# A decoder layer on one core: x split while it loads, products scaled by token after PSUM, paced loads, and the mixer's last sums kept in PSUM

## The chip, the core and the metric

One core of one Trainium2 chip runs the whole layer in one launch. TensorE (PE) multiplies, with results in PSUM; VectorE (DVE), ScalarE (ACT) and GpSimd (POOL) work beside it; transfers are issued from SyncE's queue (SP) and from POOL's. Each engine takes its own instructions in the order that the program fixed, and waits at an instruction until what it needs is there. The metric is the device time of one execution in microseconds (us), as the median of several runs.

## The reference, cut

256 tokens of width 2048, all weights float32:

```
a = rms_norm(x, g_mix_pre);  proj = a @ w_in          # 2048 -> 3*1024 + 2*1024
q, k, v: 8 heads of 128, causal attention over one block of 256, ALiBi bias
conv: val * sigmoid(gate) -> depthwise conv(31) -> LayerNorm -> silu    # 1024 channels
mixed = concat(attn, conv) @ w_out
h = x + rms_norm(mixed, g_mix_post)
f = square(relu(rms_norm(h, g_ffn_pre) @ w_ff1)) @ w_ff2               # 2048 -> 8192 -> 2048
out = h + rms_norm(f, g_ffn_post)
```

## The kernel before, in words

**Products.** All weights stream through SBUF once, in chunks of 128 x 1024 words (`load_raw`, 512 KB, four buffers `raw`). `load_w` splits a chunk into a high part `whi` (ACT, line 123) and the rest `wlo` (DVE or POOL, line 125: `low_engines` says whose turn it is), seven buffers each; activations are split in the same way, and a product is three passes, high by high, low by high and high by low. `group_cols` makes 256 columns with the weights stationary, in four chunks (lines 190 and 197); `group_rows` makes 512 columns with the tokens stationary (lines 133, 136, 137). Each group has one of two accumulators in PSUM (`acc`, tile `mm`); a third use waits until the first was read out. Smaller PSUM tiles come from four banks `aux`.

**The clock of the program.** `tick` is called after each chunk. `later(n, ...)` puts work n ticks ahead; between, each tick takes some "fillers" (`rate`), which are the 240 taps of the depthwise convolution on DVE (line 410). A scheduler then fixes the order on each engine.

**Stages.** (1) x comes in transposed, in nine pieces (`x_piece`), each with the weights of the first two column groups (gate and value of the first conv channels). These two groups multiply the unsplit `xg` = x times gain by unsplit float32 weights (`mm_words`, line 216), and so does the third group (`group_words`). Meanwhile POOL sums the squares of x. (2) `x_columns` makes the two token factors r_x, `token_rows` turns them into a row `Rx` over all tokens, and `split_x` scales xg by Rx and splits it into `xa`, of which the other groups live. (3) Five more conv groups, then twice (q, k, q, k, v) with `scores`, `weights_t`, `values` some ticks later (`ppt`: transposes of the attention weights `sc`), with the taps under it all. At the end LayerNorm and silu (`ln_1`, `ln_2`). (4) The output projection: three groups of 512 columns over the attention half of `ma`, then three over the conv half, whose sums stay in `part` (SBUF), multiplied by the gain on POOL. (5) The fourth column group, with all of the first 128 tokens (t = 0) ahead of the second 128 (t = 1): `mix_scale` makes the factor of the norm and adds each of four column blocks to `xs` (`hidden`, line 601), and `hidden_t` transposes these (`pt`, line 609) and splits them into `ha`. The transposes stand between the matmuls of the six chunks that were held back for t = 1 (`TURN_FIRST`). (6) `first_cols` starts the feed-forward with t = 0 alone for six chunks (`TURN_SECOND` places the transposes of t = 1 there), then comes the rest: four quarters of w_ff1 and w_ff2.

POOL also issues three kinds of transfer: `gains` (4 x 256 KB), all of x as `xs` (2 MB) and `gbc_ffn` (1 MB).

Of the kernel before, what the change touches and what calls it, by code (L numbers as in the profile page):

```python
# [38 lines left out]
def tile_hybrid_layer(  # L39
# [73 lines left out]

    def load_w(nk, width):
# [104 lines left out]
    def group_words(a):  # L219
        ps = acc()  # L220
        for c in range(KD // 4):
            mm_words(ps, a, 4 * c, 4, c == 0, c == KD // 4 - 1)
            tick()
        return ps[:, :, :S]

# [93 lines left out]

# [5 lines left out]
    def x_piece(k0, nk):  # L325
        at, to = KD + k0 * S if k0 else 0, KD + (k0 + nk) * S
        tc.keep_in_program_order(nc.sync.dma_start(xraw[:, at:to], xt[:, at:to]))
        v = xraw[:, to - nk * S:to].rearrange("p (k s) -> p k s", k=nk)
        for j in range(nk):
            nc.vector.tensor_scalar_mul(xg[:, k0 + j, :], v[:, j, :], xraw[:, k0 + j:k0 + j + 1])  # L330
# [19 lines left out]
    def x_columns():  # L350
        p = aux("pss")
# [89 lines left out]
    later(1, split_x)  # L441
# [17 lines left out]
    def head_cols(ps, scale, tag):  # L459
        return merged(ph1, ps, ph1.tile([P, 2, S], F32, tag=tag, name=tag), scale)  # L460

    def scores(pair, qT, kT, pT):
# [19 lines left out]
        later(3, weights_t, sc, pT)  # L482
# [36 lines left out]
    def ln_2():  # L519
# [15 lines left out]
        with tc.issue_after(last.ins):
            nc.scalar.activation(warm, eps4, AF.Sqrt)
        for b in range(4):
            split(ma, GC + 2 * b, 2, ysq[:, 2 * b:2 * b + 2, :])
# [9 lines left out]
    for half in range(2):  # L548
        pTs = []
        for b in range(2):  # L550
            qT = head_cols(group_cols(xa), HD ** -0.5, "qT")
            kT = head_cols(group_cols(xa), 1.0, "kT")
# [5 lines left out]
        nc.scalar.activation(v, ps, AF.Copy)  # L558
# [6 lines left out]
    for n in range(4):  # L565
        nc.gpsimd.dma_start(gains[n], g_mix_post[:, n * G:(n + 1) * G].to_broadcast([P, G]))
# [19 lines left out]
    part.append(mg)  # L586
# [73 lines left out]
    def first_done(ps):  # L660
# [4 lines left out]
        nc.gpsimd.dma_start(gbc_ffn, g_ffn_post.to_broadcast([P, D]))  # L665
# [69 lines left out]
RATE = (2, 5, 4)  # L735
GATE_AT = 5
# [4 lines left out]
TURN_SECOND = ((), (), (), (0,), (1,), (2, 3))  # L741
# [79 lines left out]
```

## Time and profile before

| | |
|---|---|
| median of 3 runs | 1067.19 us (1066.45 to 1068.17) |
| the profiled execution | 1066.0 us |
| its span, first to last instruction | 1064.2 us |
| PE busy / DVE / ACT / POOL | 1048.5 / 662.4 / 500.9 / 227.6 us |
| granted TensorE clock over the span | 0.998 |
| read from HBM | 199.39 MB, 189 GB/s over the span |

The span and some 2 us around it make the profiled execution's time. A busy PE is a PE with a matmul under way, by ends that are modelled; what it waited for stands in the view of waits.

### The profile page before, as it was taken

To read this page: it belongs to the slowest core of one execution; us is meant where nothing else is said; L and a number is where in the kernel's file an instruction comes from. 1 tells how busy PE (TensorE), PEld (TensorE's weight loads), DVE (VectorE), ACT (ScalarE), POOL (GpSimd) and SP (SyncE) were. 2 spreads that over 40 slices of the span, in tenths; PEclk is the share of its full clock that TensorE was granted. 3 is DMA by queue.
4 is the path that set the end of the run, shared out by engine and by line. 5 is a ranking of instruction groups with operands and counts; after the bars stand their busy time and mean duration, and the time that the engine had idled before them with its cause. 6 is when DMAs were issued, how large, how long until landed. Compare 5 with 4: busy or idle time off the path is not lost.

```text
span 1064.2 us, 14143 instructions
## 1 busy us (share of the span) xinstructions
PE 1048.5 (99%) x5424; PEld 896.1 (84%) x5424; DVE 662.4 (62%) x855; ACT 500.9 (47%) x646; POOL 227.6 (21%) x148
## 2 busy tenths in 40 slices
PE   9999999999999999999999999999999999999996
PEld 8888888888787988888888888888888888888886
DVE  4579999866465776644466654556665546656554
ACT  0465455468455754444445443344443334444450
POOL 6699755300025310000001100000010000100111
PEclk9999999999999999999999999999999999999999
DMA  7667645554764565655566655656656555566642
GB/s 226 219 216 234 219 146 191 185 173 140 285 195 137 199 214 196 195 190 190 193 194 184 194 187 194 196 184 195 194 181 196 197 192 186 190 190 194 189 149 79
DMA packets 58403, 202.41 MB, mean 190 GB/s; under 512 B 6496, under 2 KB 8416, under 8 KB 57952
## 3 DMA queue, kind: packets, MB, share of 16 engines
q1 hardware_dynamic: 57600, 197.32, 57.4%
q0 software_dynamic: 736, 4.19, 1.1%
q8 instruction: 42, 0.69, 0.2%
q14 instruction: 25, 0.20, 0.0%
HBM read 199.39 MB, written 2.10 MB: 189 GB/s over the span
## 4 chain that ended last, share of the span: by engine, by line
PE 85%; DVE 6%; POOL 3%; ACT 3%; DMA 2%; issue 2%; DVEq 0%; ACTq 0%; POOLq 0%
PE mm L190 25%; PE mm L133 14%; PE mm L137 14%; PE mm L136 14%; PE mm L197 13%; PE mm L216 3%; POOL wlo L125 3%; DVE yp L410 3%; DMA raw<-in_weights_dram 2%; DVE wlo L125 1%; DVE xs L601 1%; ACT whi L123 1%; PE half L137 0%; PE half L136 0%; PE half L133 0%
## 5 line engine op out<-in xcount | busy, mean ns | idle before, releaser
L125 DVE TENSOR_TENSOR wlo<-raw,whi 128x1024 fp32r<-128x1024 f32 x299 | 382.4, 1280 | 288.3 <-ACT whi L123 287.9
L123 ACT ACTIVATE whi<-raw 128x1024 fp32r<-128x1024 f32 x356 | 376.0, 1058 | 383.6 <-PE mm L137 216.6
L190 PE MATMUL mm<-ha,whi 128*128 128x512 f32 (+1 forms) x1072 | 317.8, 385 | 0.0
L197 PEld LDWEIGHTS mm<-ha,wlo 128*128 128x128 f32 x1024 | 186.4, 188 | 40.4
L197 PE MATMUL mm<-ha,wlo 128*128 128x256 f32 x1024 | 197.1, 279 | 0.0
L136 PE MATMUL mm<-wlo,ua 128*128 128x512 f32 x496 | 193.0, 389 | 0.0
L133 PE MATMUL mm<-whi,ua 128*128 128x512 f32 x496 | 193.0, 389 | 0.0
L137 PE MATMUL mm<-whi,ua 128*128 128x512 f32 x496 | 193.0, 389 | 0.0
L190 PEld LDWEIGHTS mm<-ha,whi 128*128 128x128 f32 x1072 | 164.3, 189 | 2.9 <-DVE mg L596 0.2
L650 POOL TENSOR_TENSOR rl<-rl 128x512 f32<-128x512 f32 x32 | 39.4, 1231 | 570.6 <-ACT ua L649 570.6
L125 POOL TENSOR_TENSOR wlo<-raw,whi 128x1024 fp32r<-128x1024 f32 x57 | 139.2, 2462 | 50.3 <-ACT whi L123 44.7
L190 PE MATMUL mm<-xa,whi 128*128 128x512 f32 x416 | 129.9, 397 | 0.0
L410 DVE SCALAR_TENSOR_TENSOR yp<-yx,cols,yp 128x256 f32<-128x256 f32 x240 | 105.8, 483 | 6.2 <-ACT yp L406 3.0
L137 PEld LDWEIGHTS mm<-whi,ua 128*128 128x128 f32 x496 | 93.1, 188 | 19.4
L136 PEld LDWEIGHTS mm<-wlo,ua 128*128 128x128 f32 x496 | 93.1, 188 | 19.3
L133 PEld LDWEIGHTS mm<-whi,ua 128*128 128x128 f32 x496 | 93.1, 188 | 19.2
L197 PEld LDWEIGHTS mm<-xa,wlo 128*128 128x128 f32 x416 | 76.2, 188 | 17.0
L197 PE MATMUL mm<-xa,wlo 128*128 128x256 f32 x416 | 80.2, 279 | 0.0
L190 PEld LDWEIGHTS mm<-xa,whi 128*128 128x128 f32 x416 | 64.8, 189 | 1.2
L254 ACT ACTIVATE tb<-mm 128x512 f32<-128x512 f32 x45 | 26.8, 596 | 72.4 <-PE mm L190 72.4
L133 PE MATMUL mm<-whi,ma 128*128 128x512 f32 x128 | 50.2, 394 | 2.3 <-ACT part L573 2.3
L257 DVE SCALAR_TENSOR_TENSOR z<-mm,tb 128x512 f32<-128x512 f32 x37 | 25.6, 691 | 39.6 <-ACT tb L254 39.6
(168 smaller groups left out, 793.1 us busy)
## 6 DMA issues: line engine op xcount, KB each, us to landing
raw<-in_weights_dram SPq DMA_DIRECT2D x360, 512.0 KB, 4.1
raw<-in_weights_dram SPq DMA_DIRECT2D x14, 256.0 KB, 3.3
xs<-in_x_dram POOLq DMA_DIRECT2D x1, 2048.0 KB, 9.7
xraw<-in_xt_dram SPq DMA_DIRECT2D x7, 256.0 KB, 3.9
gains<-in_g_mix_post_dram POOLq DMA_DIRECT2D x4, 256.0 KB, 5.0
gbc_ffn<-in_g_ffn_post_dram POOLq DMA_DIRECT2D x1, 1024.0 KB, 4.9
out_dram<-fp SPq DMA_DIRECT2D x8, 128.0 KB, 2.0
out_dram<-fp SPq DMA_DIRECT2D x4, 256.0 KB, 2.3
```

The lines of the kernel that those rows point to most:

```text
L123: nc.scalar.activation(hi[:, :n], raw, AF.Copy)
L125: low_engines[0][chunks[0] % len(low_engines[0])].tensor_sub(lo[:, :n], raw, hi[:, :n].bitcast(F32))
L133: m = nc.tensor.matmul(ps, h, wh[:, j, :], start=first and j == 0, stop=False)
L136: nc.tensor.matmul(ps, h, wl[:, j, :], start=False, stop=False)
L137: nc.tensor.matmul(ps, l, wh[:, j, :], start=False, stop=last and j == nk - 1)
L190: m = nc.tensor.matmul(o[:, :, tok], wh[:, j, b * P:(b + 1) * P], a[:, ak + j, :, tok], start=st, stop=en)
L197: nc.tensor.matmul(ps[:, b, :S], wl[:, j, b * P:(b + 1) * P], a[:, ak + j, 0, :], start=False, stop=False)
L216: nc.tensor.matmul(ps[:, b, :S], w[:, j, b * P:(b + 1) * P], a[:, ak + j, :], start=first and j == 0, stop=last and j == nk - 1)
L254: nc.scalar.activation(tb, ps[:, :, S:], AF.Copy, scale=scale)
L257: nc.vector.scalar_tensor_tensor(z, ps[:, :, :S], scale, tb, op0=ALU.mult, op1=ALU.add)
L410: nc.vector.scalar_tensor_tensor(yp[0][:, b, :], hpad[:, g + b, k:k + S], tap_col(g + b, k), yp[0][:, b, :], op0=ALU.mult, op1=ALU.add)
L650: nc.gpsimd.tensor_mul(t, t, t)
```

## The change

**x.** Each piece is now split as it comes in, into the high and low part of x times gain, without the token factor (`high` on ACT, `low` on DVE; xg itself moves to ACT from the third block on). `split_x` is gone. Since the token factor is the same for all rows of a product's column, every product of xa is multiplied by Rx after it left PSUM: `scaled` merges the two halves of a group into a PSUM tile `zt` and `by_token` multiplies this by Rx into SBUF. The v groups, which have tokens on partitions, take r_x as ACT's scale. The two `z` copies of the first groups go to `zt` tiles too.

**Third group.** `group_words` is gone; the gate of the second pair of conv blocks goes through `group_cols` like the others, on split weights.

**Loads.** `gains`, `xs` and `gbc_ffn` are issued on SP's queue among the weights, in pieces of 256 KB, one every few ticks.

**Mixer.** `part` of t = 0 is copied to three PSUM banks (`pc0`), from which `hidden` reads; the last block is multiplied by its gain in place in PSUM, and `hidden` reads it there, for both halves of the tokens.

**Order.** The LayerNorm's last step and silu come in two halves, a tick apart (`swish`); `weights_t` comes after 4 ticks instead of 3; filler rates 5 and 4 become 4.7 and 3.7; POOL takes 4 low parts of 5 instead of 3 of 4 in the attention stage; the transposes of t = 1 stand a chunk later.

```diff
+    def by_token(zt, tag="z", bufs=3):
+        z = ph1.tile([P, 2, S], F32, tag=tag, name=tag, bufs=bufs)
+        nc.vector.tensor_mul(z, zt, over(Rx, 2))
+        return z
+    def scaled(ps, scale=1.0, **kw):
+        return by_token(merged(ph1, ps, aux("zt").rearrange("p (b s) -> p b s", b=2), scale), **kw)
...
         for j in range(nk):
-            nc.vector.tensor_scalar_mul(xg[:, k0 + j, :], v[:, j, :], xraw[:, k0 + j:k0 + j + 1])
+            if k0 < 2:
+                nc.vector.tensor_scalar_mul(xg[:, k0 + j, :], v[:, j, :], gains[j])
+            else:
+                nc.scalar.activation(xg[:, k0 + j, :], v[:, j, :], AF.Copy, scale=gains[j])
+        for j in range(nk):
+            high(xa, k0 + j, v[:, j, :], gains[j], slice(0, S))
+        for j in range(nk):
+            low(xa, k0 + j, v[:, j, :], gains[j], slice(0, S))
...
-    def split_x():
-        R = token_rows(r_x, Rx)
-        for k in range(0, KD, 2):
-            xn = aux("xn").rearrange("p (k s) -> p k s", k=2)
-            nc.vector.tensor_mul(xn, xg[:, k:k + 2, :], over(R, 2))
-            split(xa, k, 2, xn)
...
-    ps = group_words(xg)
-    z = ph1.tile([P, 2, S], F32, tag="z", name="z", bufs=3)
-    nc.vector.tensor_mul(z, ps, over(Rx, 2))
-    low_engines[0], rate[0] = (nc.gpsimd,), RATE[1]
+    rate[0] = RATE[1]
     for i in range(1, 4):
-        sig = gate_out(z if i == 1 else merged(ph1, group_cols(xa)), 2 * i)
-        value_out(merged(ph1, group_cols(xa)), 2 * i, sig)
-    low_engines[0], rate[0] = (nc.vector, nc.gpsimd, nc.gpsimd, nc.gpsimd), RATE[2]
+        zg = scaled(group_cols(xa))
+        low_engines[0] = (nc.gpsimd,)
+        sig = gate_out(zg, 2 * i)
+        value_out(scaled(group_cols(xa)), 2 * i, sig)
+    low_engines[0], rate[0] = (nc.vector,) + 4 * (nc.gpsimd,), RATE[2]
...
-        nc.gpsimd.dma_start(gains[n], g_mix_post[:, n * G:(n + 1) * G].to_broadcast([P, G]))
+        later(2 * n + 10, load, gains[n], g_mix_post[:, n * G:(n + 1) * G].to_broadcast([P, G]))
...
-    nc.gpsimd.dma_start(xs, x2.rearrange("(t p) d -> p t d", p=P))
+    for n in range(8):
+        t, cs = n // 4, slice(n % 4 * G, (n % 4 + 1) * G)
+        later(n + 6, load, xs[:, t, cs], x2[t * P:(t + 1) * P, cs])
...
+        first_half.append(aux("pc0"))
+        nc.scalar.activation(first_half[c], pc[:, 0, :], AF.Copy)
...
         for c in range(3):
-            hidden(t, r, c)
-        tc.keep_in_program_order(nc.vector.tensor_mul(mg[:, t, :], ps, gains[3]))
-        hidden(t, r, 3)
+            hidden(t, r, c, part[c][:, t, :] if t else first_half[c])
+        tc.keep_in_program_order(nc.vector.tensor_mul(ps, ps, gains[3]))
+        hidden(t, r, 3, ps)
...
-RATE = (2, 5, 4)
-GATE_AT = 5
+RATE = (2, 4.7, 3.7)
+GATE_AT = 3
-TURN_SECOND = ((), (), (), (0,), (1,), (2, 3))
+TURN_SECOND = ((), (), (), (), (0,), (1, 2, 3))
```

ACT's order where the first two groups end. Before, from its start (`z` are the two copies that free the accumulators of these groups, `y_x` belongs to the token factors, `xn` is the scaled x):

```order
L65 ACTIVATE warm<-eps_75 128x1
L383 ACTIVATE z<-mm 128x512 x2
L270 ACT_TABLE_LOAD
L270 ACTIVATE y_x_279<-ssx,eps_75 128x1
L270 ACTIVATE y_x_290<-ssx,eps_75 128x1
L123 ACTIVATE whi<-raw 128x1024
L389 ACTIVATE xa<-xn 128x2x256 x3
```

Now, from the last piece of x on:

```order
L338 ACTIVATE xg<-xraw 128x256 x2
L316 ACTIVATE xa<-xraw 128x256 x2
L127 ACTIVATE whi<-raw 128x1024
L396 ACTIVATE zt<-mm 128x512
L127 ACTIVATE whi<-raw 128x1024
L396 ACTIVATE zt<-mm 128x512
L127 ACTIVATE whi<-raw 128x1024 x2
```

The first two `whi` now stand each ahead of one of the two copies.

DVE's order in the mixer, at t = 1 (`part` are the sums of blocks 0 to 2, `mm` the last block, `ha` the low parts after the transposes). Before:

```order
L601 SCALAR_TENSOR_TENSOR xs<-part,r_m_3083,xs 128x512 x3
L596 TENSOR_TENSOR mg<-mm,gains 128x512
L314 SCALAR_TENSOR_TENSOR ha<-pt,cols,ha 128x128 x2
L601 SCALAR_TENSOR_TENSOR xs<-mg,r_m_3083,xs 128x512
L314 SCALAR_TENSOR_TENSOR ha<-pt,cols,ha 128x128 x14
```

Now:

```order
L613 SCALAR_TENSOR_TENSOR xs<-part,r_m_3179,xs 128x512 x3
L608 TENSOR_TENSOR mm<-mm,gains 128x512
L319 SCALAR_TENSOR_TENSOR ha<-pt,cols,ha 128x128 x2
L613 SCALAR_TENSOR_TENSOR xs<-mm,r_m_3179,xs 128x512
L319 SCALAR_TENSOR_TENSOR ha<-pt,cols,ha 128x128 x14
```

The rows stand alike, but the accumulator `mm` was last read by the second of them before, and is now by the fourth.

SP's order of transfers in the output projection, now (before, it holds `raw` alone from the fifth column group to the end):

```order
L111 DMA raw<-in_weights_dram 128x1024 x2
L116 DMA gains<-in_g_mix_post_dram 128x512
L111 DMA raw<-in_weights_dram 128x1024 x2
L116 DMA xs<-in_x_dram 128x512
L111 DMA raw<-in_weights_dram 128x1024
L116 DMA xs<-in_x_dram 128x512
L111 DMA raw<-in_weights_dram 128x1024
```

One piece of `xs` follows each chunk of weights, eight times in a row.

## Rows read from the trace of the kernel before

**Rows 1.** What PE waited for: total us, times, longest

```profile
PE mm L133 <- ACT part L573: 2.3, 1, 2.3
PE pt L609 <- DVE xs L601: 2.3, 3, 0.8
PE ppt L488 <- ACT sc L481: 1.1, 1, 1.1
```

**Rows 2.** Stretches: us, busy PE, PEld, DVE, ACT, POOL; PEclk, DMA share, GB/s

```profile
100.00:150.00 50.00, 48.89 (x282) 42.40 (x281) 49.01 (x102) 24.25 (x36) 31.48 (x14) 1.00 0.55 192
...
355.00:1056.00 701.00, 700.86 (x3632) 599.36 (x3631) 395.60 (x391) 313.29 (x357) 54.27 (x42) 1.00 0.59 188
```

**Rows 3.** The chain in order of time: one column group after another

```profile
393.90 0.93 PE mm L190 x4
405.07 0.93 PE mm L190 x4
```

**Rows 4.** PE in order of time, 0 to 60 us

```profile
8.44 24.48 PE L216 MATMUL mm<-xg,raw 128*128 128x256 f32 x112 [0.47 <-DMA raw<-in_weights_dram]
...
33.12 5.86 PE L216 MATMUL mm<-xg,raw 128*128 128x256 f32 x26
...
47.05 0.81 PE L190 MATMUL mm<-xa,whi 128*128 128x512 f32 x2
```

**Rows 5.** Tile raw, 27.5 to 33.5 us: issues, and time to landing

```profile
L111 SPq DMA_DIRECT2D raw<-in_weights_dram x4: 328/328/328, 27.8 to 33.0; - x4
...
DMA to landing us min/median/max: 4.4/4.5/4.6
```

**Rows 6.** Groups by line and form: count | busy us, mean ns | idle before

```profile
L123 ACT ACTIVATE whi<-raw 128x1024 fp32r<-128x1024 f32 x356 | 376.0, 1058 | 383.6 <-PE mm L137 216.6 <-PE mm L190 127.9 <-DMA raw<-in_weights_dram 33.5
...
L383 ACT ACTIVATE z<-mm 128x512 f32<-128x512 f32 x2 | 1.2, 597 | 30.1 <-PE mm L216 30.1
...
L125 DVE TENSOR_TENSOR wlo<-raw,whi 128x1024 fp32r<-128x1024 f32 x299 | 382.4, 1280 | 288.3 <-ACT whi L123 287.9
...
L125 POOL TENSOR_TENSOR wlo<-raw,whi 128x1024 fp32r<-128x1024 f32 x57 | 139.2, 2462 | 50.3 <-ACT whi L123 44.7
...
L451 DVE TENSOR_TENSOR z<-mm,Rx 128x512 f32<-128x512 f32 x1 | 0.7, 683 | 0.0
```

**Rows 7.** The wait at 148 us: PE's, DVE's and ACT's rows

```profile
148.44 0.33 PE L488 MATMUL ppt<-ident,sc 128*128 128x128 f32 x1 [1.11 <-ACT sc L481]
...
131.05 0.68 DVE L257 SCALAR_TENSOR_TENSOR kT<-mm,tb 128x512 f32<-128x512 f32 x1
...
125.59 0.60 ACT L254 ACTIVATE tb<-mm 128x512 f32<-128x512 f32 x1 [1.92 <-PE mm L190]
```

**Rows 8.** Before the wait at 274 us: ACT's rows, the landings, the big load

```profile
273.93 1.06 ACT L123 ACTIVATE whi<-raw 128x1024 fp32r<-128x1024 f32 x1 [6.92 <-DMA raw<-in_weights_dram]
...
DMA to landing us min/median/max: 8.5/8.9/9.0
...
xs<-in_x_dram POOLq DMA_DIRECT2D x1, 2048.0 KB, 9.7
```

**Rows 9.** DVE in the mixer, in order of time

```profile
335.34 6.35 DVE L601 SCALAR_TENSOR_TENSOR xs<-part,r_m,xs 128x512 f32<-128x512 f32 x3
341.61 0.68 DVE L596 TENSOR_TENSOR mg<-mm,gains 128x512 f32<-128x512 f32 x1
...
349.41 2.08 DVE L601 SCALAR_TENSOR_TENSOR xs<-part,r_m,xs 128x512 f32<-128x512 f32 x3
...
352.08 0.61 DVE L314 SCALAR_TENSOR_TENSOR ha<-pt,cols,ha 128x128 fp32r<-128x128 f32 x2
352.61 0.74 DVE L601 SCALAR_TENSOR_TENSOR xs<-mg,r_m,xs 128x512 f32<-128x512 f32 x1
```

**Rows 10.** POOL and PE in the mixer, in order of time

```profile
335.91 13.21 POOL L125 TENSOR_TENSOR wlo<-raw,whi 128x1024 fp32r<-128x1024 f32 x5 [4.13 <-ACT whi L123]
...
346.42 3.98 PE L190 MATMUL mm<-ha,whi 128*128 128x256 f32 x32
```

More of the change, by code (lines that the diff above doesn't have):

```diff
@@ L112, in load_raw, with load @@
         return raw[:, :n]
+    def load(dst, src):
+        tc.keep_in_program_order(nc.sync.dma_start(dst, src))
     def load_w(nk, width):
@@ L217, in mm_words @@
                                  start=first and j == 0, stop=last and j == nk - 1)
[L219 to L224, printed above, removed]
     def first_cols(a, during, done):
@@ L328, in x_piece @@
         v = xraw[:, to - nk * S:to].rearrange("p (k s) -> p k s", k=nk)
+        gains = [xraw[:, k0 + j:k0 + j + 1] for j in range(nk)]
         for j in range(nk):
-            nc.vector.tensor_scalar_mul(xg[:, k0 + j, :], v[:, j, :], xraw[:, k0 + j:k0 + j + 1])
+            if k0 < 2:
[6 more added lines that the diff above has]
+            low(xa, k0 + j, v[:, j, :], gains[j], slice(0, S))
         sq = ph1.tile([P, 4, S], F32, tag=("v", "pT")[k0 // 4 % 2], name="xsq", bufs=2)
@@ L350, in x_columns @@
     def x_columns():
+        nc.scalar.activation(warm, eps4, AF.Sqrt)
         p = aux("pss")
@@ L374, in first_groups @@
         ps = (acc(), acc())
-        z = [ph1.tile([P, 2, S], F32, tag="z", name="z", bufs=3) for _ in range(2)]
+        z = [aux("zt").rearrange("p (b s) -> p b s", b=2) for _ in range(2)]
         k = 0
@@ L432, in glu @@
     def glu(zg, zv, g):
-        for z in (zg, zv):
-            nc.gpsimd.tensor_mul(z, z, over(Rx, 2))
+        zg, zv = by_token(zg), by_token(zv)
         value_out(zv, g, gate_out(zg, g))
@@ L440, in tile_hybrid_layer @@
     x_columns()
-    later(1, split_x)
+    later(2, token_rows, r_x, Rx)
     distances()
@@ L481, in scores @@
             nc.scalar.activation(s, s, AF.Copy, scale=sm[:, h, t:t + 1])
-        later(3, weights_t, sc, pT)
+        later(4, weights_t, sc, pT)
     def weights_t(sc, pT):
@@ L530, in ln_2, with swish @@
         nc.vector.tensor_mul(rs, rs, tn)
-        nc.vector.tensor_mul(y, y, over(rs, GC))
-        for g in range(GC):
+        later(1, swish, rs, 0)
+        later(2, swish, rs, GC // 2)
+    def swish(rs, g0):
+        gs = slice(g0, g0 + GC // 2)
+        nc.vector.tensor_mul(y[:, gs, :], y[:, gs, :], over(rs, GC // 2))
+        for g in range(g0, g0 + GC // 2):
             last = nc.scalar.activation(ysq[:, g, :], y[:, g, :], AF.Silu,
                                         bias=col("lnb", g), scale=col("lng", g))
[L535 to L538, printed above, removed]
+        if g0:
+            with tc.issue_after(last.ins):
+                nc.scalar.activation(warm, eps4, AF.Sqrt)
+        for g in range(g0, g0 + GC // 2, 2):
+            split(ma, GC + g, 2, ysq[:, g:g + 2, :])
     def normalise():
@@ L557, in tile_hybrid_layer @@
         v = ph1.tile([P, NT, G], F32, tag="v", name="v", bufs=2)
-        nc.scalar.activation(v, ps, AF.Copy)
+        for t in range(NT):
+            nc.scalar.activation(v[:, t, :], ps[:, t, :], AF.Copy, scale=r_x[t])
         later(1, values, half, pTs, v)
@@ L574, in tile_hybrid_layer @@
         part.append(pc)
-    mg = ph1.tile([P, NT, G], F32, tag="pT", name="mg", bufs=2)
     xs = apool.tile([P, NT, D], F32, tag="yx", name="xs")
-    nc.gpsimd.dma_start(xs, x2.rearrange("(t p) d -> p t d", p=P))
+    for n in range(8):
+        t, cs = n // 4, slice(n % 4 * G, (n % 4 + 1) * G)
+        later(n + 6, load, xs[:, t, cs], x2[t * P:(t + 1) * P, cs])
     ssq = [stat.tile([P, 4], F32, name=f"ssq{t}") for t in range(NT)]
+    first_half = []
     for c in range(3):
@@ L594, in mix_scale, with hidden @@
         for c in range(3):
-            hidden(t, r, c)
-        tc.keep_in_program_order(nc.vector.tensor_mul(mg[:, t, :], ps, gains[3]))
-        hidden(t, r, 3)
-    def hidden(t, r, c):
+            hidden(t, r, c, part[c][:, t, :] if t else first_half[c])
+        tc.keep_in_program_order(nc.vector.tensor_mul(ps, ps, gains[3]))
+        hidden(t, r, 3, ps)
+    def hidden(t, r, c, src):
         hs = xs[:, t, c * G:(c + 1) * G]
-        nc.vector.scalar_tensor_tensor(hs, part[c][:, t, :], r, hs, op0=ALU.mult, op1=ALU.add)
+        nc.vector.scalar_tensor_tensor(hs, src, r, hs, op0=ALU.mult, op1=ALU.add)
     def hidden_t(t, c):
@@ L664, in first_done @@
         gbc_ffn = ph2.tile([P, D], F32, name="gbc_ffn")
-        nc.gpsimd.dma_start(gbc_ffn, g_ffn_post.to_broadcast([P, D]))
+        for n in range(4):
+            cs = slice(n * G, (n + 1) * G)
+            later(4 * n + 40, load, gbc_ffn[:, cs], g_ffn_post[:, cs].to_broadcast([P, G]))
         fp = ph2.tile([P, NT, D], F32, name="fp")
```

7 lines of the change are left out of this document (2 added, 5 removed).

## The prediction, on record before the changed kernel ran

> **What bounds the kernel now.** I read the stretches first. From 355 to 1056 us PE is busy 700.86 of 701 us [rows 2], and the change adds or removes no matmul there: nothing can be won behind 355 us, and only a new wait could lose. The chain in order of time gives the pace to which PE can be held: one column group, four chunks, follows the other after 405.07 - 393.90 = 11.17 us [rows 3]. Ahead of 355 us two things are left: matmuls that cost more than this pace, and waits. The first is the third group on unsplit float32 words: it runs from 33.12 to 47.05 us, 13.93 us in place of 11.17 [rows 4]. The view of waits then names three places: 2.3 us for ACT's copy `part`, 2.3 us in three pieces for DVE's `xs` in the mixer, 1.1 us for the attention weights [rows 1]. Together these are 2.76 + 5.7 = 8.5 us: that is all that the change can win, and each piece has its own give-back.
>
> **1. The third group, and the handover to it.** The group takes 11.17 us on split weights, so 2.76 us less; the two transposes for Rx stand in it before and after. In the words stage xg is ready no later than now: ACT, idle for 30.1 us there [rows 6], takes over most of it. But split weights have to be split. The first full chunk is issued at 27.8 us and lands 4.5 us later [rows 5], at 32.25; its issue depends on PE giving back a buffer, which does not change. `whi` takes 1.06 us, so it ends at 33.3; DVE's `wlo` takes some 1.25 us more, 34.6 [rows 6]. In the new ACT order the first `zt` copy (0.60 us, [rows 6]) stands behind this `whi`: it ends at 33.9, and only then is the accumulator free that the third group writes. Before, that copy had been made long before PE needed it. PE ends the words at 8.44 + 24.48 = 32.92 us [rows 4], so it waits 1.0 us for the copy and, after two matmuls of the high part, some 0.4 us for `wlo`. Later chunks have more lead (2.79 us of PE each, against 1.06 of ACT and 1.25 of DVE). The term is 2.76 - 1.4 = **1.3 us**. Bounds: 2.7 if nothing of this shows; 0 if DVE's first `wlo` is held up by POOL (part 4 shows by how much) once.
>
> **2. The attention weights.** The transposes `ppt` came 1.11 us too early for the softmax [rows 7]. The reason is DVE's backlog: the copy that frees kT's group started on ACT at 125.59 and DVE came to the sum at 131.05, some 5 us late [rows 7], in a stretch where DVE was busy 49.01 of 50 us [rows 2]. The change takes seventeen wide DVE operations (eight multiplications by Rx and eight subtractions in `split_x`, one behind `group_words`) out of the time just before the taps. It adds eleven up to this place: two for the first pair, which POOL made before, six for the other conv groups, three for q and k. The one that exists took 0.68 us [rows 6]; at that price for all, DVE has 17 - 11 = 6 operations, 4.1 us, less to do. The sixteen low parts of x that replace the subtractions lie under the loads, ahead of all taps. If half of the 4.1 us counts, the backlog shrinks by 2 us, more than the wait: **1.1 us**. Bounds: 1.1 and, if the backlog stays, 0.
>
> **3. The big load.** ACT sat 6.92 us on a chunk of weights, and `part` stood behind it; the four chunks issued around 265 us took 8.5 to 9.0 us to land where 4.4 to 4.6 was seen above, since the 2 MB of `xs` were issued a microsecond earlier and took 9.7 us [rows 5, 8]. Now `xs` goes in eight pieces, one between two chunks of weights. A piece is half a chunk; the DMA share is 0.55 to 0.59 with chunks alone [rows 2], so 0.9 with a piece to each, and the four raw buffers are as many chunks of lead. A chunk that lands after 4.5 us lets ACT go on some 4 us earlier, and the wait was 2.3: **2.3 us**. Bound on the other side: 0, if the chunk was late because ACT had silu and its table loads to do before it.
>
> **4. The mixer.** At t = 0 three additions `xs` took 6.35 us, 2.1 each, while POOL made low parts; at t = 1 the same three took 2.08 us, 0.69 each, half a microsecond after POOL had ended (335.91 + 13.21 = 349.12) [rows 9, 10]. An operation with one operand in PSUM is not slowed: multiplying the accumulator by the gain took 0.68 us at 341.61, amid POOL's low parts [rows 9, 10]. So at t = 0, with operands now in PSUM, the additions should take 0.69 each, and PE's three waits (2.3 us) go.
>
> The page "SBUF — State Buffer" of the Trainium skill, in "SBUF: two separate sides", says why: a DVE operation with both inputs in SBUF and a GpSimd operation that reads SBUF lock each other out for a whole instruction. The rows agree (2.1 against 0.69 us).
>
> But t = 1 still reads `part` in SBUF, and it now comes sooner. PE began the feed-forward at 346.42 and DVE the additions of t = 1 at 349.41, 3.0 us later [rows 9, 10]; now PE is there at 346.4 - 2.3 = 344.1, and the additions could begin 2 to 3 us later (2 if DVE has no low parts of t = 0 left to make), at 346.1 to 347.1. POOL's five low parts begin when they did, at 335.91, since they wait for nothing that is sooner, and at their mean of 2.46 us [rows 6] end at 348.2. So one or two of the additions wait for POOL to end an instruction, and the third ends between 348.7 and 350.0; before it was 351.5 (349.41 + 2.08). Then come the multiplication 0.68, two low parts 0.6 and the last addition 0.7 us [rows 9], and by the new order only this last frees the accumulator that the fifth chunk of the feed-forward needs. Before, the multiplication freed it, at 352.08. Now it is free at 350.7 to 352.0, so of the 2.3 us won PE keeps 0.1 to 1.4: **0.7 us**. Bounds: 2.3 if POOL is not in the way; -1 if all three additions are held.
>
> By that page's rule the additions at t = 1 take whole instructions of POOL, which is the 0.7; without it they would take 0.69 each and the term would be 2.3.
>
> **5. At nothing.** `gbc_ffn` in pieces, POOL's share of the low parts, silu in halves and the copies `pc0` lie under PE's busy time; the cover is the lead of seven split chunks. The end, from the last matmul on, is untouched.
>
> **The sum.** 1.3 + 1.1 + 2.3 + 0.7 = 5.4 us off the profiled execution's 1066.0, that is 1060.6. The median of the runs shown, 1067.19, lies 1.2 us above that execution; carried over, the forecast is **1061.8 us**.
>
> **Rivals.** (a) No give-back: the handover is smooth and POOL is done in time. Then 2.76 + 1.1 + 2.3 + 2.3 = 8.5, so 1058.7. For it: the order was made by a scheduler that leaves PE few waits now. Against: three additions that waited on POOL are in the rows. (b) `part` is still late: ACT had silu and its table loads to make just before, and holds the raw buffers meanwhile. Then 1061.8 + 2.3 = 1064.1. (c) No change: the handover costs all of the third group's gain and more, the mixer gives back 1 us more than it wins, and one of the two other waits stays: 0 - 1 + 2.3, so 1065.9. (d) Slower: DVE in the conv stage. It is full there (49.01 of 50), and the multiplications by Rx now stand between a group's end and what waits for it. If what was removed only filled idle time ahead of the taps, the eleven that are added, 7.5 us, come on top of the backlog. `ppt`, which PE takes at the same place between its matmuls, then waits 1.1 + 7.5 = 8.6 us: 1061.8 + 8.6 = 1070.4. It decides from a wait of 5.4 us on. Against it: the operations removed stood right ahead of the first tap, on the same engine, and outnumber those added.
>
> **How the numbers follow.** The forecast has 0.58, (a) 0.15, (b) 0.12, (c) 0.09, (d) 0.06. The measurement can tell 0.2% from no change, that is 2.1 us; the forecast, (a) and (b) lie beyond it: faster 0.85, same 0.09 (c), slower 0.06 (d). The range leaves out (c) and (d) and half of (a)'s lower end: 1058.6 to 1064.8, which holds (b) and, at its top, only one of the three waits won.
>
> **What the profile would show.** PE's first `mm<-xa` near 33.9 us and the next group near 45.7: part 1. No `ppt <- sc` among the waits: part 2. Landings of 4 to 6 us near 265 us and no `part` there: part 3. Additions at t = 0 of 0.7 us, at t = 1 of 2 us, and a wait of the feed-forward's fifth chunk for `xs`: part 4. The forecast is wrong if a new name stands in the waits ahead of 355 us, above all `psc`, `pav` or `mm` for DVE.

## The result and the profile after

The changed kernel takes 1060.3 us (median of 4 runs, 1059.89 to 1060.73), the kernel before, timed beside it, 1067.51 (1066.45 to 1068.17): a ratio of 0.9935, with a 95% interval of 0.9922 to 0.9948, or 5.6 to 8.3 us less. The profiled execution took 1059.89 us, with a span of 1058.1 in place of 1064.2: 6.1 us less, where 5.4 were forecast. The rows below are from these two executions.

What PE waited for in the changed kernel (total us, times, longest); the rows answer to [rows 1]:

```profile
PE mm L194 <- DVE xs L613: 1.2, 1, 1.2
...
PE pt L621 <- DVE xs L613: 1.0, 1, 1.0
PE mm L194 <- ACT zt L396: 0.8, 1, 0.8
```

`part` and `ppt` are gone. `pt` still waits for `xs`, but at t = 1 of the mixer in place of t = 0, and for 1.0 us in place of 2.3. Two waits are new: for the copy `zt` at the handover, and for the accumulator of the feed-forward's fifth chunk. The changed kernel's rows in order of time, at the places of [rows 4, 7, 9, 10] (start, duration, in brackets the idle time before and what ended it):

```profile
32.10 1.06 ACT L127 ACTIVATE whi<-raw 128x1024 fp32r<-128x1024 f32 x1 [4.12 <-DMA raw<-in_weights_dram]
33.07 0.58 ACT L396 ACTIVATE zt<-mm 128x512 f32<-128x512 f32 x1
33.70 0.73 PE L194 MATMUL mm<-xa,whi 128*128 128x512 f32 x2 [0.81 <-ACT zt L396]
34.48 0.50 PE L201 MATMUL mm<-xa,wlo 128*128 128x256 f32 x2
...
45.48 1.08 PE L194 MATMUL mm<-xa,whi 128*128 128x512 f32 x4
...
53.68 6.78 DVE L416 SCALAR_TENSOR_TENSOR yp<-yx,cols,yp 128x256 f32<-128x256 f32 x13
...
124.29 0.60 ACT L251 ACTIVATE tb<-mm 128x512 f32<-128x512 f32 x1 [1.92 <-PE mm L194]
124.92 0.70 DVE L254 SCALAR_TENSOR_TENSOR zt<-mm,tb 128x512 f32<-128x512 f32 x1 [0.40 <-ACT tb L251]
...
145.64 0.28 PE L489 MATMUL ppt<-ident,sc 128*128 128x128 f32 x1
...
265.83 1.03 ACT L581 ACTIVATE part<-mm 128x1024 f32<-128x1024 f32 x1 [1.66 <-PE mm L141]
...
329.80 2.07 DVE L613 SCALAR_TENSOR_TENSOR xs<-pc,r_m,xs 128x512 f32<-128x512 f32 x3
...
330.48 11.85 POOL L129 TENSOR_TENSOR wlo<-raw,whi 128x1024 fp32r<-128x1024 f32 x5 [4.18 <-issue]
...
337.97 4.00 PE L194 MATMUL mm<-ha,whi 128*128 128x256 f32 x32
340.75 3.46 DVE L613 SCALAR_TENSOR_TENSOR xs<-part,r_m,xs 128x512 f32<-128x512 f32 x3
342.94 1.98 PE L621 MATMUL pt<-ident,xs 128*128 128x128 f32 x12 [0.97 <-DVE xs L613]
344.13 0.69 DVE L608 TENSOR_TENSOR mm<-mm,gains 128x512 f32<-128x512 f32 x1
...
345.33 0.74 DVE L613 SCALAR_TENSOR_TENSOR xs<-mm,r_m,xs 128x512 f32<-128x512 f32 x1
...
346.13 2.17 PE L194 MATMUL mm<-ha,whi 128*128 128x256 f32 x16 [1.21 <-DVE xs L613]
```

Read them by place. *Start:* `whi` ends at 33.1, `zt` behind it at 33.65, PE starts at 33.70. *Attention:* the sum for kT follows its `tb` after 0.63 us (5.46 before), and `ppt` has no wait. *Mixer:* the additions of t = 0 take 0.69 us each; those of t = 1 begin at 340.75, before POOL is done at 342.33, and take 3.46 us for three (2.08 before), one by one 2.13, 0.74 and 0.74; the fifth chunk starts when the last addition has freed the accumulator, at 346.07. Landings of the four chunks issued from 261.4 us on, to be read against the 8.5 to 9.0 us of [rows 8]:

```profile
DMA to landing us min/median/max: 3.5/5.0/6.1
```

Beside these four, two 256 KB pieces of `gains` were issued, at 264.1 and 266.4 us. The pieces of `xs` come later, from 270.8 to 289.9 us, and the chunks issued among them landed after 3.9 to 5.4 us.

And the stretch that answers to 355:1056 of [rows 2], busy times as there:

```profile
349.00:1050.00 701.00, 700.82 (x3632) 599.28 (x3631) 395.08 (x387) 312.64 (x356) 53.45 (x42) 1.00 0.59 188
```

Nothing changed there, as forecast. PE's lead over the kernel before, from the starts of the same matmul in both, gives the size of each part:

| up to | before | after | lead | of this part | forecast |
|---|---|---|---|---|---|
| the fifth column group (part 1) | 58.39 | 57.09 | 1.30 | 1.30 | 1.3 |
| the first v group (part 2) | 151.22 | 148.41 | 2.81 | 1.51 | 1.1 |
| the first transposes of t = 0 (part 3) | 336.15 | 330.60 | 5.55 | 2.74 | 2.3 |
| the feed-forward's second pass (part 4) | 354.51 | 348.50 | 6.01 | 0.46 | 0.7 |

### The profile page after: what moved, and what is told of

It reads as the page before. It is cut to its first block, busy times and chain, and to the rows that moved or that the text cites. A ratio compares the mean times of both kernels' runs of the same rounds, so it can differ in the third digit from the quotient of the medians.

```text
span 1058.1 us, 14197 instructions
## 1 busy us (share of the span) xinstructions
PE 1045.0 (99%) x5424; PEld 893.8 (84%) x5424; DVE 658.0 (62%) x859; ACT 515.8 (49%) x678; POOL 226.5 (21%) x143
## 4 chain that ended last, share of the span: by engine, by line
PE 97%; DVE 1%; ACT 1%; DMA 1%; issue 0%; DVEq 0%; ACTq 0%
PE mm L194 32%; PE mm L201 16%; PE mm L140 15%; PE mm L141 15%; PE mm L137 15%; PE mm L220 2%; DMA raw<-in_weights_dram 1%; ACT whi L127 0%; DVE xs L613 0%; ACT ha L316 0%; PE half L141 0%; PE half L140 0%; PE half L137 0%; PE psc L470 0%; PE pav L498 0%; PE warm L74 0%
## 5 line engine op out<-in xcount | busy, mean ns | idle before, releaser
L127 ACT ACTIVATE whi<-raw 128x1024 fp32r<-128x1024 f32 x360 | 381.1, 1059 | 378.6 <-PE mm L141 212.6
L129 POOL TENSOR_TENSOR wlo<-raw,whi 128x1024 fp32r<-128x1024 f32 x60 | 143.3, 2433 | 63.1 <-ACT whi L127 53.1
L194 PE MATMUL mm<-xa,whi 128*128 128x512 f32 x448 | 140.3, 398 | 0.8 <-ACT zt L396 0.8
L201 PEld LDWEIGHTS mm<-xa,wlo 128*128 128x128 f32 x448 | 82.0, 188 | 18.6 <-DVE wlo L129 0.5
L201 PE MATMUL mm<-xa,wlo 128*128 128x256 f32 x448 | 87.2, 280 | 0.0
L194 PEld LDWEIGHTS mm<-xa,whi 128*128 128x128 f32 x448 | 69.7, 189 | 2.5 <-ACT zt L396 1.2
L251 ACT ACTIVATE tb<-mm 128x512 f32<-128x512 f32 x46 | 27.5, 598 | 79.5 <-PE mm L194 79.5
L140 PE MATMUL mm<-wlo,ma 128*128 128x512 f32 x128 | 49.8, 389 | 0.0
```

What stands on the lines that cost most here:

```text
L140: nc.tensor.matmul(ps, h, wl[:, j, :], start=False, stop=False)
L194: m = nc.tensor.matmul(o[:, :, tok], wh[:, j, b * P:(b + 1) * P], a[:, ak + j, :, tok], start=st, stop=en)
L201: nc.tensor.matmul(ps[:, b, :S], wl[:, j, b * P:(b + 1) * P], a[:, ak + j, 0, :], start=False, stop=False)
```

## The experiments

Each was timed in 5 or more runs (e8 in 4) beside the kernel before, whose medians there were 1066.06 (e1 to e4), 1066.57 (e5 to e8) and 1066.55 us (e9 to e12). The changed kernel itself was not timed again there. The kernels e3 and e9, whose traces show its waits, by name and within 0.1 us, came to 1060.02 and 1060.17, so 1060.2 stands for it. The intervals of the ratios of e1 to e4, e8, e9 and e11 overlap with its own, 0.9922 to 0.9948; what tells such a kernel from the changed one is the places in the traces, with the medians beside them. "Second pass" is the start of the feed-forward's second pass, 348.50 in the changed kernel.

### e1: the last block of t = 1 through SBUF

```diff
+    mg = ph1.tile([P, G], F32, tag="sc", name="mg", bufs=2)
-        tc.keep_in_program_order(nc.vector.tensor_mul(ps, ps, gains[3]))
-        hidden(t, r, 3, ps)
+        dst = mg if t else ps
+        tc.keep_in_program_order(nc.vector.tensor_mul(dst, ps, gains[3]))
+        hidden(t, r, 3, dst)
```

> The changed kernel, but at t = 1 the last block is multiplied by its gain into an SBUF tile, as before the change, and no longer in place; t = 0 stays in PSUM. Theory: of the wait of the feed-forward's fifth chunk, 1.2 us, all is the accumulator, which is freed only by the last addition (346.07 us) and would be freed by the multiplication (344.8). Then this chunk starts at 344.9 in place of 346.13, the second pass at 347.3 in place of 348.50, and the time falls by 1.2 us, from 1060.3 to 1059.1. Rival: what PE waits for is the transposed tokens of t = 1, late in any case because of the additions; then the wait only changes its name and the time stays at 1060.3.

1058.6 us, ratio 0.9931 (0.9917 to 0.9944); second pass at 347.21. In order of time:

```profile
344.11 0.68 DVE L610 TENSOR_TENSOR mg<-mm,gains 128x512 f32<-128x512 f32 x1
...
344.84 2.18 PE L194 MATMUL mm<-ha,whi 128*128 128x256 f32 x16
```

The fifth chunk starts when the multiplication has read the accumulator (344.79), with no wait. All of the 1.2 us was the accumulator.

### e2: two low parts away from POOL

Two chunks put their low part on a list (`late`), which DVE takes up behind twelve transposed blocks of t = 1 (`lows`).

```diff
+            w = load_w(4, 2 * P, late if n in (3, 4) else None)
...
+                with tc.issue_after(lows[-5].ins):
+                    while late:
+                        late.pop(0)()
-    low_engines[0] = (nc.gpsimd,)
+    low_engines[0] = [nc.gpsimd if (n - chunks[0] - 1) % 8 in (0, 1, 2, 5, 6, 7) else nc.vector for n in range(8)]
```

> The changed kernel, but the low parts of the fourth and fifth chunk of the feed-forward are made on DVE behind twelve of the transposed blocks of t = 1, instead of on POOL; POOL makes three in a row there in place of five and is done near 337.8 us. Theory: the three additions of t = 1 (340.75 us, 3.46 us for three) are held by POOL's fifth low part; without it they take 2.1 us, the first transposes of t = 1 wait 0 in place of 1.0 us, and the second pass starts near 347.1 in place of 348.50: 1.4 us less, 1058.9. Rival 1: the additions are slow for another reason than POOL (ACT reads the same memory); then they still take 3.4 us and the time is 1060.3. Rival 2: the two low parts on DVE, 2.5 us, come too late for the second pass, which waits for them: above 1060.3.

1059.01 us, ratio 0.9932 (0.992 to 0.9944); second pass at 347.59, in a run whose start was 0.3 us later. In order of time:

```profile
341.04 2.08 DVE L626 SCALAR_TENSOR_TENSOR xs<-part,r_m,xs 128x512 f32<-128x512 f32 x3
...
342.08 1.75 PE L634 MATMUL pt<-ident,xs 128*128 128x128 f32 x12
345.21 2.19 PE L202 MATMUL mm<-ha,whi 128*128 128x256 f32 x16 [1.39 <-DVE xs L626]
```

Without POOL the same three additions take 2.08 us, and the transposes don't wait. The wait for the accumulator stays, as it must.

### e3: x for the mixer in one transfer again

```diff
-    for n in range(8):
-        t, cs = n // 4, slice(n % 4 * G, (n % 4 + 1) * G)
-        later(n + 6, load, xs[:, t, cs], x2[t * P:(t + 1) * P, cs])
+    nc.gpsimd.dma_start(xs, x2.rearrange("(t p) d -> p t d", p=P))
```

> The changed kernel, but all of x for the mixer comes in one transfer of 2 MB from POOL's queue, as before the change; gains and the last gain vector stay in pieces. Theory: the large transfer shares the engines with four chunks of weights, these land after 8.5 to 9 us in place of 4 to 6, ACT stands at a chunk and part comes late: a wait of 2.3 to 2.5 us is back, 1062.7. Rival: the order on ACT (silu now in halves) removed that wait; then the chunks land late, but ACT has nothing behind them that PE needs at once, and the time stays at 1060.3.

1060.02 us, ratio 0.9942 (0.9929 to 0.9954): no loss. From the first v group to the first `pt` PE takes 182.20 us, in the changed kernel 182.19. ACT's rows:

```profile
265.40 1.03 ACT L581 ACTIVATE part<-mm 128x1024 f32<-128x1024 f32 x1 [1.66 <-PE mm L141]
...
270.38 1.03 ACT L581 ACTIVATE part<-mm 128x1024 f32<-128x1024 f32 x1 [3.02 <-PE mm L141]
...
275.62 1.06 ACT L127 ACTIVATE whi<-raw 128x1024 fp32r<-128x1024 f32 x1 [3.26 <-DMA raw<-in_weights_dram]
```

and the landings of the six chunks issued from 260.9 us on:

```profile
DMA to landing us min/median/max: 3.5/8.8/11.3
```

The chunks came later than ever, and ACT waited for one. But the first two `part` stood ahead of that chunk, and PE, which lived from chunks already split, waited for none. My theory fell here: in the changed kernel the pacing isn't what frees `part`.

### e4: the third group on unsplit words

```diff
-        zg = scaled(group_cols(xa))
+        zg = by_token(group_words(xg)) if i == 1 else scaled(group_cols(xa))
```

> The changed kernel, but the third group multiplies unsplit words again, as before the change, with its products multiplied by Rx; the other groups live on the split x. Theory: the group costs 2.76 us more, and the handover (0.98 us for the copy, 0.2 for the low part, 0.4 for the sums of squares that now stand inside) is gone: 1.1 to 1.3 us more, 1061.5. Rival: with a smooth handover the first column groups start from a fuller store of chunks, and the whole 2.76 - 1.3 is got back at a later wait: 1060.3; or the full difference of 2.8 shows: 1063.1.

1061.48 us, ratio 0.9956 (0.9943 to 0.9968): some 1.2 us more. From the end of the first two groups to the fifth group's start PE takes 25.64 us (33.06 to 58.70), in the changed kernel 24.37 (32.72 to 57.09): 1.27 us. Part 1 stands as forecast.

### e5: the kernel before, with x for the mixer paced

```diff
-    nc.gpsimd.dma_start(xs, x2.rearrange("(t p) d -> p t d", p=P))
+    for n in range(8):
+        t, cs = n // 4, slice(n % 4 * G, (n % 4 + 1) * G)
+        later(n + 6, load, xs[:, t, cs], x2[t * P:(t + 1) * P, cs])
```

> The kernel before, with one edit: x for the mixer comes in eight pieces on SP's queue, one behind each of eight chunks of weights, and not in one transfer of 2 MB. The order on ACT is that of before, with part behind a chunk that came late. Theory (the prediction's third part): the chunks land after 4 to 6 us, the wait of ACT at 267 us falls from 6.9 to some 2 us, PE's wait for part, 2.5 us, is gone, and the time falls by 2.5 us against the kernel before. Rival: the wait comes from ACT, which made silu and its table loads just ahead and so gave the raw buffers back late; then ACT still waits some 6 us at that chunk and the time is that of before.

1063.56 us (1061.68 to 1064.3), ratio 0.9964 (0.9952 to 0.9977). ACT's order is that of before:

```profile
269.38 1.06 ACT L127 ACTIVATE whi<-raw 128x1024 fp32r<-128x1024 f32 x1 [1.66 <-PE mm L141]
272.11 1.03 ACT L577 ACTIVATE part<-mm 128x1024 f32<-128x1024 f32 x1 [1.66 <-PE mm L141]
```

The chunk that ACT awaited 6.92 us [rows 8] is there; no `part` among PE's waits; from the first v group to `pt` PE takes 182.31 us in place of 184.93, 2.62 less.

### e6: the kernel before, with silu in halves

```diff
-        nc.vector.tensor_mul(y, y, over(rs, GC))
-        for g in range(GC):
...
+        later(1, swish, rs, 0)
+        later(2, swish, rs, GC // 2)
```

> The kernel before, with one edit: the last step of the LayerNorm and silu come in two halves, a tick apart; x still comes in one transfer of 2 MB. On ACT a chunk is now split between the two halves, and two more ahead of part. Theory, after the run in which the large transfer was put back into the changed kernel and cost nothing: what keeps part from being late there is the order on ACT, and the halves make it; then PE's wait for part is gone here too, 2.5 us less than before, although chunks still land after 8 to 9 us. Rival: the halves alone don't move part ahead of the late chunk, and the wait stays at 2 us or more.

1065.69 us, ratio 0.9988 (0.9979 to 0.9997). PE's waits:

```profile
PE pt L615 <- DVE xs L607: 2.3, 3, 0.8
PE ppt L488 <- ACT sc L481: 1.1, 1, 1.1
...
PE mm L133 <- ACT ma L389: 1.0, 1, 1.0
```

`part` is gone from them with the transfer unpaced, as the theory had it. But `ma` came late in its place (1.0 us, and 0.3 for its low part), and from the v group to `pt` only 0.81 us is left of 2.5. The expectation, all of the 2.5, was missed.

### e7: sixteen operations ahead of the taps

```diff
+    def extra():
+        for k in range(0, KD, 2):
+            xn = aux("xn").rearrange("p (k s) -> p k s", k=2)
+            nc.vector.tensor_mul(xn, xg[:, k:k + 2, :], over(Rx, 2))
+            nc.vector.tensor_sub(xn, xg[:, k:k + 2, :], xn)
+    later(2, extra)
```

> The changed kernel, with sixteen wide operations added on DVE where split_x stood (eight products of xg and Rx and eight differences, into PSUM, read by nobody). Theory (the prediction's second part): DVE is full from the first tap on, so what stands ahead of the taps shifts all behind them; the first tap comes some 9 us later than 53.7, the order gives back 12 taps (5.8 us), so the sum for kT at 125 us comes 3 to 5 us late in place of 0.6, the attention weights are ready at 147 to 149 in place of 144.3, and PE, which takes them at 145.6, waits 1.5 to 3.5 us: 1061.8 to 1063.8. Rival: DVE's idle time further on takes it up (it has 2 us at 40 to 50 us and little later), or the rates set the lateness; then no ppt wait and 1060.3.

1073.42 us, ratio 1.0062 (1.0049 to 1.0074), far beyond both, and at another place:

```profile
50.89 11.21 DVE L451 TENSOR_TENSOR xn<-xg,Rx 128x512 f32<-128x512 f32 x4
...
63.93 0.99 ACT L429 ACTIVATE sig<-z,cols 128x256 f32<-128x256 f32 x2 [7.09 <-DVE xn L452]
...
68.42 1.19 PE L194 MATMUL mm<-xa,whi 128*128 128x512 f32 x2 [11.12 <-ACT tb L251]
```

Products of two SBUF inputs took 2.8 us each while POOL made low parts; `sig` waited for a PSUM bank that such a tile held, `tb` stood behind `sig` on ACT, and PE stood 11.1 us for the accumulator. This run doesn't answer the question on the taps. It raised another, which is e10.

### e8: e1 and e2 together

Both diffs above, on the changed kernel.

> The changed kernel with both mixer edits: the last block of t = 1 multiplied into SBUF, and the fourth and fifth low part made on DVE after the transposed blocks. Theory: the two waits are in series, 1.0 us for the first transposes of t = 1 and 1.2 us for the accumulator, so both go: second pass at 346.2 in place of 348.50, 2.2 us less, 1058.0. Rival: each edit alone already took the larger part (1.3 and 1.2 us), since both waits end in the same row of DVE work, and what is left is the transposed blocks of t = 1 on ACT; then 1058.7.

1057.29 us, ratio 0.9909 (0.9894 to 0.9925); second pass at 345.61, 2.9 us sooner, of which 0.25 is a start that was sooner; 2.2 were expected. In order of time:

```profile
340.50 2.08 DVE L628 SCALAR_TENSOR_TENSOR xs<-part,r_m,xs 128x512 f32<-128x512 f32 x3
...
341.55 1.74 PE L636 MATMUL pt<-ident,xs 128*128 128x128 f32 x12
343.23 2.19 PE L202 MATMUL mm<-ha,whi 128*128 128x256 f32 x16
```

No wait of PE is left in the mixer. This kernel is faster than e1 and e2 alone, and its median lies 3 us under the changed kernel's.

### e9: every product with Rx made twice

```diff
-        nc.vector.tensor_mul(z, zt, over(Rx, 2))
+        for _ in range(2):
+            nc.vector.tensor_mul(z, zt, over(Rx, 2))
```

> The changed kernel, with each multiplication by Rx on DVE made twice (13 more operations of 0.68 us with one input in PSUM and one in SBUF, and nothing behind them but themselves). Up to kT's sum nine more stand ahead, 6.1 us, and the order puts nine taps (4.4 us) behind it. Theory (the prediction's second part, mended by the run with the late taps: DVE is full, but the order moves taps away from what PE waits for): the sum for kT comes some 2.4 us late in place of 0.6, the weights are ready near 146 us, PE waits 0 to 0.5 us there, and the time is 1060.3 to 1061.3. Rival (d) of the prediction: all of the 6 to 8 us comes on top of the backlog, and ppt waits 5 us or more: above 1065.

1060.17 us, ratio 0.9936 (0.9924 to 0.9949). The rows show sixteen more operations, not 13; 10.9 us of DVE cost nothing:

```profile
125.18 0.70 DVE L254 SCALAR_TENSOR_TENSOR zt<-mm,tb 128x512 f32<-128x512 f32 x1 [0.70 <-ACT tb L251]
```

The sum for kT comes 0.63 us behind its `tb` (124.55), as without them. The first tap is at 54.08. Nine of the sixteen stand ahead of kT's sum, and nine taps went behind it in the order (131 stood ahead, now 122); DVE even waited 0.70 us for `tb`.

### e10: zt in SBUF

```diff
-        return by_token(merged(ph1, ps, aux("zt").rearrange("p (b s) -> p b s", b=2), scale), **kw)
+        z = ph1.tile([P, 2, S], F32, tag="zs", name="zs", bufs=2)
+        return by_token(merged(ph1, ps, z, scale), **kw)
```

> The changed kernel, but the merged halves of a group (zt) stand in SBUF and not in PSUM, so that the multiplication by Rx has both inputs in SBUF; nothing else is changed, and no operation is added. Theory: while POOL makes low parts (all of 46 to 200 us), such an operation waits for POOL's instruction, as the additions at t = 0 did before the change (2.1 us each) and as the added products of xg and Rx did in the run with the late taps (2.1 to 2.8 us); eleven of them ahead of kT cost 1.4 to 2.1 us more each, 15 to 20 us on a full DVE, and PE waits 8 to 20 us in all: 1068 to 1080. Rival: the merged tile is read between two of POOL's instructions most of the time, the multiplications take 0.7 to 1.0 us, and the time is 1060.3 to 1062.

1063.76 us, ratio 0.9978 (0.9966 to 0.9989): 3.6 us more, between the two. Groups by line and form (count, busy us, mean ns), here:

```profile
L259 DVE TENSOR_TENSOR z<-zs,Rx 128x512 f32<-128x512 f32 x6 | 8.1, 1345 | 0.0
L259 DVE TENSOR_TENSOR qT<-zs,Rx 128x512 f32<-128x512 f32 x4 | 4.9, 1235 | 0.0
L259 DVE TENSOR_TENSOR kT<-zs,Rx 128x512 f32<-128x512 f32 x4 | 4.5, 1124 | 0.0
```

in the changed kernel:

```profile
L259 DVE TENSOR_TENSOR z<-zt,Rx 128x512 f32<-128x512 f32 x8 | 5.4, 685 | 0.1
```

and, in order of time in e10:

```profile
120.93 2.88 DVE L259 TENSOR_TENSOR qT<-zs,Rx 128x512 f32<-128x512 f32 x1
...
124.68 0.60 ACT L251 ACTIVATE tb<-mm 128x512 f32<-128x512 f32 x1 [1.92 <-PE mm L194]
...
130.78 0.68 DVE L254 SCALAR_TENSOR_TENSOR zs<-mm,tb 128x512 f32<-128x512 f32 x1
...
134.22 0.49 PE L470 MATMUL psc<-kT,qT 128*128 128x128 f32 x2 [1.21 <-DVE kT L259]
148.61 0.33 PE L490 MATMUL ppt<-ident,sc 128*128 128x128 f32 x1 [1.64 <-ACT sc L483]
```

The products take 1.12 to 1.35 us on the mean, up to 2.88. The sum for kT is 6.1 us late, and `ppt` waits again. One by one, seven of the fourteen began inside one of POOL's low parts and ended 0.55 to 0.56 us after it; four began as POOL was between two and took 0.68 to 0.69 us, and POOL's next low part then took 2.9 us in place of 2.4; three ran with POOL idle. The expectation of 8 to 20 us had the size wrong, since it held every product for 1.4 to 2.1 us, and the mechanism right. The Trainium skill, page "SBUF — State Buffer", section "SBUF: two separate sides", states that a DVE operation with two SBUF inputs and a GpSimd operation that reads SBUF exclude each other, and that the one that starts first keeps the other out for its whole instruction. These times agree.

### e11: the mixer as before

```diff
-            hidden(t, r, c, part[c][:, t, :] if t else first_half[c])
-        tc.keep_in_program_order(nc.vector.tensor_mul(ps, ps, gains[3]))
-        hidden(t, r, 3, ps)
+            hidden(t, r, c, part[c][:, t, :])
+        tc.keep_in_program_order(nc.vector.tensor_mul(mg[:, t, :], ps, gains[3]))
+        hidden(t, r, 3, mg[:, t, :])
```

> The changed kernel with the mixer of before: no copies pc0, the additions of t = 0 read part in SBUF, the last block goes through SBUF for both halves. Theory: PE's three waits of 2.3 us at t = 0 are back, and the two at t = 1 (1.0 and 1.2 us, with the rows around them 2.0 us more than before) are gone, since t = 1 comes 2.4 us later and POOL is done: 0.5 us more, 1060.8. Rival: the waits at t = 1 have nothing to do with coming sooner, and stay; then 2.3 us more, 1062.6.

1060.6 us, ratio 0.9942 (0.9929 to 0.9955). PE's waits have one name in the mixer:

```profile
PE pt L619 <- DVE xs L611: 2.3, 3, 0.8
```

Second pass at 349.16, 0.6 us later than in the changed kernel once the start (0.1 us later) is taken off. So the mixer part alone is worth 0.5 to 0.6 us, with its give-back; by the medians it is 0.3 to 0.4, too little for them to show.

### e12: e8, and the handover smoothed

On top of e8:

```diff
-                    nc.scalar.activation(z[g], ps[g][:, :, :S], AF.Copy)
+                    if g:
+                        nc.scalar.activation(z[g], ps[g][:, :, :S], AF.Copy)
+                    else:
+                        nc.vector.tensor_copy(z[g], ps[g][:, :, :S])
...
+                if highs and fn is with_low:
+                    later_lows.append(fn)
+                    continue
...
+        for fn in later_lows:
+            fn(0)
+            fn(1)
...
-        zg = scaled(group_cols(xa))
+        zg = scaled(group_cols(xa, highs=i == 1))
```

> The changed kernel with both mixer edits, and at the handover to split weights the first zt copy made on DVE, which is idle there, and the eight high passes of the first chunk ahead of its low passes. Theory (the prediction's first part): PE waits there 0.98 us for the copy behind the first split chunk and 0.3 to 0.4 us for the low part; now the first wait is for the split chunk alone (ready at 33.3 us, 0.6 us) and the low part comes in time, 0.7 us less than with the mixer edits alone: 1056.6. Rival: the first chunk lands later than its split can use, so that both orders end at the same low part; then 1057.3.

1056.76 us (1056.47 to 1057.66), ratio 0.9907 (0.9894 to 0.992); e8 had 1056.99 to 1057.38. PE's start:

```profile
34.43 2.11 PE L203 MATMUL mm<-xa,whi 128*128 128x512 f32 x8 [0.54 <-ACT whi L127]
```

The wait is now for the split chunk itself, and the low passes don't wait. But from the end of the words to the fourth group's start it is 12.65 us, in e8 12.77, in the changed kernel 13.22: when the first chunk lands against the words' end varies by as much as the edit was to win. Inconclusive; e8 and e12 can't be told apart.

## Why the prediction was right, step by step

**The bounds.** Right: nothing moved behind 355 us, and of the 8.5 us at stake 6.0 came. The 8.5 was a little low: the profiled execution of e8 lies 9.0 us under that of before. The view of waits counts from modelled ends; from one matmul's start to the next, `ppt` cost 1.27 us in place of 1.11 and `part` 2.49 in place of 2.33.

**1. Third group, 1.3 us.** Right in size and working. `whi` ended at 33.1, `zt` at 33.65 and PE started at 33.70, against 33.3, 33.9 and 33.9. e4 undoes the part alone and shows 1.27.

**2. Attention weights, 1.1 us.** The effect was right and larger: kT's sum came 4.8 us less late behind its `tb`, PE gained 1.5 us (1.27 is the gap at `ppt`, the rest stays open). The step that failed is the reason, six operations fewer on a full DVE; that the size came near is luck. In e9 sixteen more cost nothing. And the count was off. Of the products nine stand ahead of kT's sum, not eleven, and the traces show five operations more that the count leaves out: a merge and four low parts for the third group, which is now split. So ahead of the sum DVE lost 17 x 0.68 = 11.6 us of work and got 10 x 0.69 + 4 x 1.23 = 11.8 us.

What moved is the first tap, from 58.46 to 53.68 us: 4.8 of the 6.1 us by which kT's sum came sooner (131.05 to 124.92). The other 1.35 us went between the two, where two taps fewer stand and DVE's three low parts took 5.3 us in place of 8.9. DVE's rows of the kernel before, just there:

```profile
55.52 0.87 DVE L428 SCALAR_TENSOR_TENSOR yx<-z,cols,sig 128x256 f32<-128x256 f32 x2 [3.31 <-ACT sig L423]
58.46 3.64 DVE L410 SCALAR_TENSOR_TENSOR yp<-yx,cols,yp 128x256 f32<-128x256 f32 x7 [2.06 <-ACT yp L406]
```

and of the changed kernel:

```profile
51.55 0.87 DVE L434 SCALAR_TENSOR_TENSOR yx<-z,cols,sig 128x256 f32<-128x256 f32 x2 [5.89 <-ACT sig L429]
```

DVE stood idle for ACT just ahead of the taps, 5.4 us before and 5.9 now. The gate's input `z` was ready long before that, at 42.3 us (POOL's products) and 45.7 us (DVE's), so the place of `sig` in ACT's order decides when the taps begin. Before, ACT split `split_x`'s tiles until 51.5 us and made the first two pairs of `sig` from 52.8 to 55.4; in the changed kernel it makes the first from 50.1 to 51.5. Two edits can have moved that place: `split_x`'s copies are gone, and `GATE_AT` calls the first gate after 3 ticks in place of 5, which the prediction didn't consider. No run moved either alone, so the cause of the earlier taps stays open between them. That a late kT brings the wait back is shown by e10: 6.1 us late, and 1.64 us at `ppt`. Rival (d) had a premise that was true (DVE was idle ahead of the taps), and yet the doubled products cost nothing: the order put nine taps behind kT's sum. e10 shows what (d) would have needed: the operand in SBUF.

**3. The big load, 2.3 us.** Right in size: 2.74 in the changed kernel, 2.62 in e5, where the pacing stands alone and the chunks land after 4.5 us at the median. But pacing worked otherwise than the step has it. The step reckons with a piece beside each of these chunks, a DMA share of 0.9; in fact the first piece of `xs` goes out at 270.8 us (275.7 in e5), after ACT has begun the first `part` (265.8; 272.1 in e5). The 2 MB were out of the way. Nor is pacing the only cause. The wait needs a `part` that stands on ACT behind a chunk issued after the big transfer. Before, the transfer went out at 263.92 us, and the seventh chunk behind v, which stands ahead of `part`, at 264.92; it landed at 273.82. The change takes away both: the 2 MB come later, and by the new order two chunks in place of one are split between v and silu, so that `part` stands six chunks behind v. Either is enough: in e5 the pacing, in e3 what is left of the change without it. In e6 `part` is seventh again, but that chunk was issued at 263.91, ahead of the transfer (264.78), and landed after 3.6 us. So undoing the pacing costs nothing, and a term that is right when the edit is made alone is not what its removal costs. Rival (b) was wrong: `part` was not late. Its suspect was real in e6: halving silu frees `part` too, and hands most of the gain back to `ma`.

**4. The mixer, 0.7 us.** Right, 0.46 in the leads and 0.5 to 0.6 in e11. The path was right too: with PE's lead of 5.55 us added, the additions of t = 1 began at 346.3 us (forecast 346.1 to 347.1), the third ended at 349.8 (348.7 to 350.0), and the accumulator was free at 351.6 (350.7 to 352.0). PE won 2.9 us up to the feed-forward's start (346.42 to 337.97, less the lead of 5.55) and gave back 2.4. Both causes were as put: POOL's last low part holds the additions of t = 1 (e2: 3.46 falls to 2.08 us without it), and the accumulator is freed only by the last addition (e1: 1.2 us). Not forecast was that the transposes of t = 1 would wait too, 1.0 us. The 2.1 us for each addition at t = 0 is a mean of unlike ones: 0.75, 2.88 and 2.87 us in the kernel before. The two long ones, and the one of 2.13 us in the changed kernel, each ended 0.55 us after a low part of POOL. Rival (a) asked for neither; e8 shows that it was to be had with two more edits.

**5. At nothing.** Right: no wait of these names.

**The sum.** The terms came to 6.0 us in place of 5.4. The rest of the distance from 1061.8 to 1060.3 is the carrying over to medians: the profiled execution of before lay 1.2 us under its median, that of after 0.4. That 1.2 rested on three runs; beside the experiments the kernel before had medians of 1066.06 to 1066.57. Rival (c) needed a handover that takes back the third group's whole gain and a mixer that loses 1 us; e4 and e11 show neither.

## What to carry to other kernels

Where two edits each remove one wait, test each alone on the old kernel and undo each on the new one: a wait that needs a late transfer and an unlucky place in an engine's order goes with either, and the two gains don't add. When an operation is taken off the path, follow what comes sooner by it into the next engine's busy stretch, and look at which instruction frees a buffer: here an in-place product and POOL's low part gave back 2.4 of 2.9 us, and two small edits (e8) took 3 us more. Where POOL reads SBUF beside DVE, leave one input of a DVE product in PSUM: here it took 0.69 us in place of 1.1 to 1.35 on the mean.

## What was not expected of the hardware

A DVE product of 128x512 with both inputs in SBUF took anything from 0.68 to 2.88 us beside POOL's low parts (e10), by when in a low part it began; in e7, four in a row took 2.8 us each. A transfer of 2 MB on another queue stretched the landing of 512 KB chunks to 11.3 us (e3), more than the 9.0 of [rows 8], with no effect on PE, which had enough chunks already split.
